# TensorE's order in the second half of an RWKV-7 recurrence written out by the kernel, with its inverse built from blocks of 16

## The chip, the cores and the metric

One core of a Trainium2 chip. The metric is the device time of one execution in microseconds (us). A core has TensorE (PE; its weight loads are shown as PEld), VectorE (DVE), ScalarE (ACT), GpSimd (POOL) and SyncE (SP), which issues the DMAs. Each engine runs its own list of instructions in order and waits for others by semaphores.

## The reference

One step of a two-layer streaming encoder over 1024 frames of a new stream and 64 frames of a running one, width 1024, 16 heads of 64. Layer 0 mixes by a recurrence and has a SwiGLU FFN (width 2816); layer 1 has sliding-window attention and an FFN. The recurrence:

```python
def step(s, inp):
    r_t, w_t, k_t, v_t, a_t, b_t = inp
    sa = jnp.einsum('bhvk,bhk->bhv', s, a_t)
    s = s * w_t[:, :, None, :] + sa[..., None] * b_t[:, :, None, :] + v_t[..., None] * k_t[:, :, None, :]
    return s, jnp.einsum('bhvk,bhk->bhv', s, r_t)
...
s_fin, y = lax.scan(step, s0.astype(f32), seq_in)
```

Its result y is normalised per head, gated, and goes through `rw_w_o` into the residual, then the FFN: `(silu(gu[..., :D_FF]) * gu[..., D_FF:]) @ w_out`.

## The kernel before, in words

The kernel is written on a framework whose planner orders the instructions: each carries a priority (`tc.cur_priority`, smaller is sooner), and a simulated timeline decides at compile time which ready instruction each engine takes next. What comes out is a fixed list for each engine.

The frames are cut into half A (chunks 0 to 7 of 64 frames) and half B (chunks 8 to 15 and, as chunk 16, the running stream). Dense products split each f32 operand into a high and a low part and take three PE instructions, lines 433 to 435 (`Dense.mm`): high x high, high x low, low x high. Weights come in pieces of 128 x 512 (`Dense.piece`: DMA on SP, cast on ACT at line 393, difference at line 394 on DVE or, every third time, POOL), three raw buffers and six split ones. Results go to three PSUM banks (`dp`).

The recurrence is `Rwkv`. Within a chunk of 64 frames it is a set of small products in f32 (line 73 for products, line 77 for transposes; PE takes each f32 product as two instructions, a transpose as one), and only the 64 x 64 state of each head goes from chunk to chunk. Its functions:

- `prep`: loads s, k, a, r of the chunk, norms of k (16 instructions of PE, tile `p_rp<-c_bd,r_rt`), decayed copies AR and BK on DVE, ACT and POOL, the 16 matrices X = BK AR (32 PE instructions, tile G) with a mask, and the bonus.
- `prep2`: `inverse`, which turns X's strictly triangular part of each head into W, and the transposes BT of BK. The inverse lays 32 x 32 blocks of all heads side by side on the partitions (ACT copies at line 190, a transpose on DVE), runs 15 steps of back substitution two columns at a time on DVE (products at line 215, reductions at 219, mostly in two parts each), and then joins the blocks of 32 to 64 by two groups of PE products with a copy between them.
- `chain`: the path from state to state. U0 from X and the state, U = W U0, then Sp from BT and U, and the new state M = (Sp + M) PC; beside it Y, the read-out (`seen`: 8 products of the old state for even heads, 8 for odd ones, with a memset on POOL, line 281, set between them; then 16 of U).
- `post`: the norm of Y per head on DVE, ACT and POOL, four transposes on PE, the gate, and the store of z to DRAM.

`recur` runs these over a list of chunks with two priorities, one for PE and one for the rest. The first half, chunks 0 to 7 (priority 1, its `prep` and `post` at 2.5), stands beside the r, k and v projections of half B (priority 2). The second half, chunks 8 to 16 (chain at 3, inverse at 3.1, `prep` and `post` of the other engines at 4.5), stands beside the dense work of half A at priority 4: `mixed_in("A")` loads z, `mix_out("A")` multiplies it by `rw_w_o` (8 groups of products, evacuation at line 898), `normed` makes the norm (squares at line 522, a sum over partitions at 532, its spread at 549, the scaled rows at 918), and `Ffn("A", 0).main` runs 22 times `up` (two halves of 8 products, evacuation at 941 to 945) and after every second one the `down` of an earlier pair (8 groups, evacuation into hx at 962). Which PE instruction comes next, one of the recurrence or a dense one, is the planner's choice alone. After that come `F.rest`, `mixed_in("B")` and the rest of the model, which need z of half B.

Buffers that the change touches: `rt` (three, for kkr, its square and P of `prep`), `yc` (one), `f4` (two of 4 KB a partition for the inverse), the PSUM banks `rp` (two), `rc` (two) and `ry` (one).

Of the kernel before, what the change touches and what calls it, by code (L numbers as in the profile page):

```python
# [46 lines left out]


class Rwkv:

# [31 lines left out]
    def start(self):  # L82

        nc = self.nc
        self.W = self.sb.tile([128, 8, 64], F32, name="W", tag="W", bufs=1)
        nc.gpsimd.memset(self.W, 0.0)

    def prep(self, ch):

# [12 lines left out]
        S.activation(sq, kkr, AF.Square)  # L102

        pn = self.pp()[0:64, 0:16].rearrange("p (par j) -> p par j", par=2)
        for j in range(8):
            self.mm(pn[:, :, j], lhsT=sq[:, j, :], rhs=c["bd"][:, 0:128:64], start=True, stop=True)
        n4 = self.t([128, 32], "n4")
        for q in range(4):
            d = 32 * (q % 2)
            V.tensor_scalar(out=n4[32 * q:32 * q + 32].rearrange("p (g j) -> p g j", g=4),  # L110
                            in0=mid(pn[d:d + 32, q // 2, :], 4), scalar1=1e-24, scalar2=None, op0=ALU.max)
        V.reciprocal(out=n4, in_=n4)
        nl = self.t([128, 32], "nl", 3)
        V.transpose(out=nl, in_=n4)


# [23 lines left out]
        G.tensor_tensor(out=kp, in0=kp, in1=bc(c["r_k"], 64), op=ALU.mult)  # L140


        X = self.t([128, 16, 128], "G", 2)
        flat2 = lambda x: x.rearrange("p a b -> p (a b)")
        for g in range(2):
            ps = [self.pp().rearrange("p (a b) -> p a b", a=4) for _ in range(2)]
            for i in range(4):
                for par in range(2):
                    h = slice(64 * par, 64 * par + 64)
                    self.mm(ps[par][:, i, :], lhsT=flat2(BK[h, 4 * g + i]), rhs=flat2(AR[h, 4 * g + i]), start=True, stop=True)  # L150
            for par in range(2):
                V.tensor_tensor(out=X[:, 8 * par + 4 * g:8 * par + 4 * g + 4, :], in0=ps[par], in1=mid(c["mask"], 4), op=ALU.mult)

        vf = self.t([128, 8, 64], "vf", 3)
# [3 lines left out]
        V.tensor_tensor(out=flat(vf), in0=pb, in1=flat(vf), op=ALU.mult)  # L158
        return dict(AR=AR, BK=BK, X=X, PC=PC, vf=vf, nl=nl)

    def prep2(self, d):
        nc = self.nc
        V, S = nc.vector, nc.scalar
        AR, X = d["AR"], d["X"]
        d["W"] = self.inverse(X, d["nl"])

        Xh = X.rearrange("p (par j) t -> p j par t", par=2)
        V.tensor_copy(Xh[0:64, :, 0, 0:64], AR[0:64, :, 0, :])
        S.copy(Xh[0:64, :, 1, 0:64], AR[64:128, :, 0, :])
        flat2 = lambda x: x.rearrange("p a b -> p (a b)")  # L170

        BT = d["BT"] = self.t([128, 16, 64], "BT")
        for g in range(2):
            ps = self.pp()
            for i in range(4):
                self.tr(ps[:, 128 * i:128 * i + 128], flat2(d["BK"][:, 4 * g + i]), self.c["id"])
            S.copy(flat2(BT[:, 8 * g:8 * g + 8, :]), ps)

    def inverse(self, X, nl):


        nc, c = self.nc, self.c
        V, S, G = nc.vector, nc.scalar, nc.gpsimd
        W = self.W
        Xh = X.rearrange("p (par j) t -> p j par t", par=2)
        st = self.t([128, 1024], "f4", 2)
        for q in range(4):
            d = 32 * (q % 2)
            src = Xh[d:d + 32, :, q // 2, d:d + 32].rearrange("p j t -> p t j").unsqueeze(2).broadcast_to([32, 32, 4, 8])
            S.copy(st[32 * q:32 * q + 32].rearrange("p (t g j) -> p t g j", g=4, j=8), src)  # L190
        N12 = self.t([128, 8, 32], "in12")
        S.copy(N12[0:32], Xh[0:32, :, 0, 32:64])
# [16 lines left out]
        for j in range(30, 0, -2):  # L209
# [3 lines left out]
            for h, r0 in part:  # L213
                n = 4 - r0
# [39 lines left out]
        V.tensor_copy(W[64:96, :, 32:64], ps[64:96])  # L254
        return W

    def chain(self, ch, d, M):
# [9 lines left out]
        E = lambda x: x.rearrange("p (a b) -> p a b", a=8)  # L267
        Y, U0p = E(self.p([128, 512], "ry", 1)), E(self.pc())
        X, BT, W = d["X"], d["BT"], d["W"]
        heads = [(i, i // 2, slice(64 * (i % 2), 64 * (i % 2) + 64)) for i in range(16)]  # L270
        for i, j, h in heads:
            self.mm(U0p[h, j, :], lhsT=X[:, 8 * (i % 2) + j, 0:64], rhs=sv[:, i, :], start=True, stop=True)


        out = lambda j, par: Y[64 * (j % 2):64 * (j % 2) + 64, j // 2 * 2 + par, :]

# [4 lines left out]
        by = G.memset(self.t([1, 1], "by", 2), 0.0)  # L281
        U0 = self.t([128, 8, 64], "yc")
        S.copy(U0, U0p)
        Up = E(self.pc())
        for i, j, h in heads:
            self.mm(Up[h, j, :], lhsT=W[h, j, :], rhs=U0[h, j, :], start=True, stop=True)
        V.tensor_copy(svh[0:64, :, 0, :], Up[0:64])
        S.copy(svh[0:64, :, 1, :], Up[64:128])
        Sp = E(self.pc())
        for i, j, h in heads:  # L290
            self.mm(Sp[h, j, :], lhsT=BT[:, i, :], rhs=sv[:, i, :], start=True, stop=True)

# [7 lines left out]
        Mn = self.t([128, 8, 64], "M", 2)  # L300
        V.tensor_tensor(out=Mn, in0=Sp, in1=M, op=ALU.add)
        V.tensor_tensor(out=Mn, in0=Mn, in1=bc(d["PC"], 64), op=ALU.mult)
        return Mn, Y

    def post(self, ch, d, Y):
        nc, c = self.nc, self.c
        V, S, G = nc.vector, nc.scalar, nc.gpsimd
# [14 lines left out]
        G.tensor_tensor(out=sm[:, 3, :], in0=sm[:, 2, :], in1=c["power"], op=ALU.pow)  # L322
        G.tensor_tensor(out=yc, in0=yc, in1=bc(sm[:, 3, :], 64), op=ALU.mult)

        for q in range(0, 8, 2):
# [25 lines left out]
class Dense:  # L351


    def __init__(self, tc, sb, ps, c):
        self.tc, self.nc, self.sb, self.ps, self.c = tc, tc.nc, sb, ps, c
        self.n = self.turn = 0
        self.more = self.esb = None
        self.mixed = []
        self.spare, self.early = deque("x" * RING), deque()
# [69 lines left out]
    def mm(self, ps, parts):  # L429

        last = len(parts) - 1
        for i, (wh, wl, xh, xl) in enumerate(parts):
            self.nc.tensor.matmul(ps, lhsT=wh, rhs=xh, start=i == 0, stop=False)  # L433
            self.nc.tensor.matmul(ps, lhsT=wh, rhs=xl, start=False, stop=False)  # L434
            self.nc.tensor.matmul(ps, lhsT=wl, rhs=xh, start=False, stop=i == last)  # L435

    def full(self, src, xs, groups, evac):
# [135 lines left out]
def tile_stream_step(ctx: ExitStack, tc: tile.TileContext, I, O):  # L573
# [278 lines left out]
    def all(gen):  # L852
        for _ in gen:
            pass
# [138 lines left out]
    def prio(p):  # L993
        tc.cur_priority = int(p * 1000000)
# [36 lines left out]

    def recur(chunks, M, base, low):

        rw.two.at(base, base)
        d = rw.prep(chunks[0])
        rw.prep2(d)
        for i, ch in enumerate(chunks):
            nd, late = None, 0.001 * i
            if i + 1 < len(chunks):
                rw.two.at(base + 0.301 + late, low + 0.301 + late)  # L1040
                nd = rw.prep(chunks[i + 1])
            rw.two.at(base + late, base + late)
            M, Y = rw.chain(ch, d, M)
            rw.two.at(base + late, low + late)
            rw.post(ch, d, Y)
            if nd:
                rw.two.at(base + 0.1 + late, base + 0.1 + late)
                rw.prep2(nd)
            d = nd
        return M  # L1050

    M = recur(range(8), M, 1, LOW[0])
    prio(2)
# [6 lines left out]
    all(rkv("B", "k", xs["Bk"]))  # L1060
    prio(3)
    M = recur(range(8, 16), M, 3, LOW[1])
    nc.sync.dma_start(O["wkv_p"], M.rearrange("p a b -> p (a b)"))
    M = rw.t([128, 8, 64], "M", 2)
    nc.sync.dma_start(M.rearrange("p a b -> p (a b)"), I["s0"])
    M = recur([16], M, 3.5, LOW[1] + 0.4)
    nc.sync.dma_start(O["wkv_s"], M.rearrange("p a b -> p (a b)"))
    prio(4)
# [5 lines left out]
    F = Ffn("A", 0, xA, x0)  # L1074
    all(F.main())
    rctx.close()
# [351 lines left out]
```

## Time and profile before

| | |
|---|---|
| median of 3 runs | 3046.8 us (3043.08 to 3048.04) |
| profiled execution | 3042.33 us, span 3040.6 us |
| mean granted clock of PE | 0.961 |
| PE busy | 2854.4 us (94%) |
| DVE busy | 1885.7 us (62%) |
| ACT, POOL busy | 1371.7 us (45%), 920.5 us (30%) |
| line 190 (ACT copies of the inverse) | 135.8 us, 68 times |
| lines 215 and 219 (DVE steps of the inverse) | 119.4 and 98.7 us, 476 times each |

How to read it: the span is the time from the first to the last instruction of one profiled execution, the execution's own time is a little longer. Busy times of engines overlap. Ends of PE instructions are modelled, so that consecutive products overlap in the list and start-to-start distances say more than durations. A row of a group gives line, engine, operation, tiles (out <- in), count, busy time and mean, and then how long the engine stood idle before and what ended that. The granted clock is the share of full speed at which PE was allowed to run.

### The profile page before, as it was taken

The numbers are of one execution on the slowest core, as the hardware profiler recorded it, in microseconds if no ns is written. First come the engines' busy times: TensorE is split into PE (matmuls) and PEld (weight loads), VectorE is DVE, ScalarE is ACT, GpSimd is POOL, SyncE is SP. The second block draws the span as 40 slices with busy tenths as digits, with TensorE's granted clock in tenths as the row PEclk, the third lists the DMA queues.
The fourth block names the chain that finished last, engine by engine and source line by source line (L and its number), as shares of the span: only waits on it lengthen the run. The fifth ranks groups of instructions, "written<-read, shape, count | busy, mean of one in ns | idle before, by whom it ended". The sixth has DMA issues, their size and how long they took to land. (4 is left out here: it accounts for less than half of the span.)

```text
span 3040.6 us, 51529 instructions
## 1 busy us (share of the span) xinstructions
PE 2854.4 (94%) x19650; PEld 2463.5 (81%) x19650; DVE 1885.7 (62%) x3964; ACT 1371.7 (45%) x2491; POOL 920.5 (30%) x785
## 2 busy tenths in 40 slices
PE   6998888988899999999999999999999999999998
PEld 5677777876677777887789999888777888999998
DVE  8887788968998994357554333565554335533334
ACT  6866665545545542244653222344554233322222
POOL 6555124333333332224211222243111222322221
PEclk9999778988899999999999999999999999999999
DMA  4645353344232225332212222222222332322222
GB/s 145 169 124 148 112 144 93 108 118 133 78 95 88 89 69 137 100 114 80 70 49 63 84 84 84 77 85 79 65 67 74 94 94 80 105 84 84 84 84 70
DMA packets 262048, 289.10 MB, mean 95 GB/s; under 512 B 125029, under 2 KB 143973, under 8 KB 261801
## 3 DMA queue, kind: packets, MB, share of 16 engines
q1 hardware_dynamic: 261800, 285.81, 31.7%
q8 instruction: 154, 2.52, 0.4%
q14 instruction: 94, 0.76, 0.1%
HBM read 243.18 MB, written 41.16 MB: 94 GB/s over the span
## 5 line engine op out<-in xcount | busy, mean ns | idle before, releaser
L433 PE MATMUL dp<-xh,wh 128*128 128x288 f32 (+2 forms) x3480 | 1180.3, 340 | 29.2 <-DVE hx L962 11.4
L434 PE MATMUL dp<-xl,wh 128*128 128x288 f32 (+2 forms) x3480 | 1172.0, 337 | 9.7 <-POOL xl L426 6.5
L435 PE MATMUL dp<-xh,wl 128*128 128x288 f32 (+2 forms) x3480 | 1167.9, 336 | 0.0
L393 ACT CAST wh<-wr 128x512 fp32r<-128x512 f32 x730 | 446.0, 619 | 820.4 <-PE dp L434 613.5
L433 PEld LDWEIGHTS dp<-xh,wh 128*128 128x128 f32 x3480 | 665.6, 192 | 109.9 <-DVE hx L962 16.0
L434 PEld LDWEIGHTS dp<-xl,wh 128*128 128x128 f32 x3480 | 666.0, 191 | 74.6 <-issue 8.6
L435 PEld LDWEIGHTS dp<-xh,wl 128*128 128x128 f32 x3480 | 666.2, 191 | 60.3 <-issue 4.9
L394 POOL TENSOR_TENSOR wl<-wr,wh 128x512 fp32r<-128x512 f32 x243 | 340.2, 1400 | 1063.2 <-ACT wh L393 948.7
L394 DVE TENSOR_TENSOR wl<-wr,wh 128x512 fp32r<-128x512 f32 x487 | 374.6, 772 | 421.1 <-ACT wh L393 417.0
L433 PE MATMUL dp<-mh,wh 128*128 128x288 f32 (+1 forms) x808 | 254.5, 315 | 0.2 <-DVE hx L962 0.2
L435 PE MATMUL dp<-mh,wl 128*128 128x288 f32 (+1 forms) x808 | 254.0, 314 | 0.0
L434 PE MATMUL dp<-ml,wh 128*128 128x288 f32 (+1 forms) x808 | 253.8, 314 | 0.0
L962 DVE TENSOR_TENSOR a_xB<-dp,a_xB 128x288 f32<-128x288 f32 x352 | 157.7, 455 | 83.5 <-PE dp L435 82.8
L943 DVE TENSOR_TENSOR st<-st,dp 128x288 f32<-128x288 f32 (+1 forms) x132 | 70.0, 530 | 222.0 <-PE dp L435 221.6
L945 POOL TENSOR_TENSOR xl<-st,xh 128x288 fp32r<-128x288 f32 (+1 forms) x102 | 102.2, 1002 | 327.6 <-ACT xh L944 318.8
L433 PEld LDWEIGHTS dp<-mh,wh 128*128 128x128 f32 x808 | 152.5, 189 | 10.7 <-issue 3.0
L435 PEld LDWEIGHTS dp<-mh,wl 128*128 128x128 f32 x808 | 152.6, 189 | 8.5 <-issue 2.4
L434 PEld LDWEIGHTS dp<-ml,wh 128*128 128x128 f32 x808 | 152.6, 189 | 6.8 <-issue 1.1
L190 ACT COPY r_f<-r_G 32x1024 f32<-32x1024 f32 x68 | 135.8, 1997 | 37.4 <-DVE r_f L226 25.4
L962 DVE TENSOR_TENSOR hx<-dp,hx 128x512 f32<-128x512 f32 x176 | 119.7, 685 | 47.9 <-PE dp L435 47.3
L215 DVE TENSOR_TENSOR r_f<-r_f,r_f 128x60 f32<-128x60 f32 (+5 forms) x476 | 119.4, 282 | 0.5
L944 ACT CAST xh<-st 128x288 fp32r<-128x288 f32 (+1 forms) x102 | 50.2, 492 | 137.3 <-DVE st L943 136.3
(343 smaller groups left out, 3850.3 us busy)
## 6 DMA issues: line engine op xcount, KB each, us to landing
wr<-in_ffn_in SPq DMA_DIRECT2D x352, 256.0 KB
wr<-in_ffn_out SPq DMA_DIRECT2D x176, 256.0 KB
wr<-in_rkv SPq DMA_DIRECT2D x90, 256.0 KB
wr<-in_rwo SPq DMA_DIRECT2D x32, 256.0 KB
wr<-in_wq SPq DMA_DIRECT2D x32, 256.0 KB
wr<-in_wo SPq DMA_DIRECT2D x32, 256.0 KB
r_r_s<-s_s SPq DMA_DIRECT2D x17, 256.0 KB
r_sv<-s_vt SPq DMA_DIRECT2D x17, 256.0 KB
```

The source lines that it names most:

```text
L190: S.copy(st[32 * q:32 * q + 32].rearrange("p (t g j) -> p t g j", g=4, j=8), src)
L215: V.tensor_tensor(out=Z[:, h, 1:3, r0:4, 0:j], in0=Z[:, h, a, r0:4, j:j + 2].rearrange("p r c -> p c r").unsqueeze(3).broadcast_to([128, 2 ...
L393: nc.scalar.copy(h, x)
L394: (nc.gpsimd if self.turn % 3 == 0 else nc.vector).tensor_tensor(out=l, in0=x, in1=h, op=ALU.subtract)
L433: self.nc.tensor.matmul(ps, lhsT=wh, rhs=xh, start=i == 0, stop=False)
L434: self.nc.tensor.matmul(ps, lhsT=wh, rhs=xl, start=False, stop=False)
L435: self.nc.tensor.matmul(ps, lhsT=wl, rhs=xh, start=False, stop=i == last)
L943: V.tensor_tensor(out=t[o], in0=t[o], in1=p, op=ALU.mult)
L944: S.copy(a.hi[:, q], t[o])
L945: G.tensor_tensor(out=a.lo[:, q], in0=t[o], in1=a.hi[:, q], op=ALU.subtract)
L962: V.tensor_tensor(out=self.x[m][:, q], in0=p, in1=self.x[m][:, q], op=ALU.add)
```

## The change

The two halves get functions of their own. `recur_free` is the old `recur` for chunks 0 to 7. For chunks 8 to 16 a new `recur` is a generator that issues one group of the recurrence, yields the time of dense work that is to pass, and goes on. The new class `Pump` holds it: from `pump.start` on, PE's order is that in which the kernel issues the instructions (`manual_schedule` for PE alone; the other engines stay with the planner), and `Dense.mm` tells it after every three products how much dense time has gone by. Products that don't go through `Dense.mm`, those of the norms, do not tick.

```diff
+class Pump:
+    def start(self, gen, priority):
...
+            self.region = self.tc.manual_schedule(engines={mybir.EngineType.PE})
+            self.region.__enter__()
+        self.tick(0)
...
+    def tick(self, n):
+        if self.gen is None:
+            return
+        self.need -= 0.44 * n + 6
+        while self.gen is not None and self.need <= 0:
+            self.step()
...
             self.nc.tensor.matmul(ps, lhsT=wl, rhs=xh, start=False, stop=i == last)
+            if self.pump:
+                self.pump.tick(3 * ps.shape[1])
...
-LOW = (2.5, 4.5)
+LOW = 2.5
+FREE = (1.5, 5.0)
...
+    def recur(chunks, M, base, low, scale, free, ends):
...
+        us = 1000.0
+        inv, fill = low + 0.05, low + 0.2
...
+        def turns(g, v, p):
+            for gap in (1.2, 1.4, 1.2, 1.4):
+                for x in (g, v):
+                    if x and next(x, x) is not x:
+                        yield gap * scale * us
+        load(0, base)
+        yield 16 * us
+        step(gs[0], base)
+        yield 4 * us
+        rw.two.at(inv, inv)
+        yield from turns(gs[0], None, base)
+        inverse(0, base)
+        keys(0, base)
+        load(1, inv)
+        yield 12 * us
+        step(gs[1], inv)
+        yield 4 * us
+        rw.two.at(inv, inv)
+        yield from turns(gs[1], vs[0], inv)
+        inverse(1, inv)
+        old = None
+        for i, ch in enumerate(chunks):
+            g, v = None, vs.get(i + 1)
+            k = rw.chain(ch, ds[i], M)
+            step(k, base)
+            yield 1.8 * scale * us
+            step(k, base)
+            if old:
+                step(old, fill)
+            yield 1.8 * scale * us
+            step(k, base)
+            M = ds[i]["M"]
+            if i + 1 < len(chunks):
+                yield scale * us
+                keys(i + 1, inv)
+            if i + 2 < len(chunks):
+                load(i + 2, inv)
+                g = gs[i + 2]
+            yield 2 * scale * us
+            step(k, base)
+            yield 1.6 * scale * us
+            step(k, base)
...
+            old = rw.post(ch, ds[i])
+            step(old, fill)
+            yield 2 * scale * us
+            if g:
+                step(g, inv)
+                yield 2 * scale * us
+            rw.two.at(inv, inv)
+            yield from turns(g, v, inv)
+            if i + 2 < len(chunks):
+                inverse(i + 2, inv)
+            yield free * us
+        step(old, fill)
...
-    M = recur(range(8), M, 1, LOW[0])
+    M = recur_free(range(8), M, 1, LOW)
...
+    pump.start(recur(range(8, 17), M, 3, 4, *FREE, {
+        15: saved, 16: lambda M: nc.sync.dma_start(O["wkv_s"], M.rearrange("p a b -> p (a b)"))}), 3)
```

`prep`, `chain` and `post` become generators that stop between their groups of PE instructions. In `prep` the products for the norms of k come after the rest of the DVE work; in `chain`, for both halves, the new state is issued before the read-out, and U0 takes a buffer of `rt` instead of `yc`. `turned` is the part of `prep2` that makes BT (`keys` calls it).

The second half takes a new `inverse16` in the place of `inverse` (which stays, as `inverse32`, for the first). It lays blocks of 16 on the partitions, two masks of which are made once at the start (`self.e`, `self.xl`), needs 7 steps of one product and one reduction each, and joins 16 to 32 by two groups of 32 products on PE, and 32 to 64 as before:

```diff
+        for j in range(14, 0, -2):
+            a, b = (0, 3) if j % 4 else (3, 0)
+            r0, n = j // 2, 8 - j // 2
+            V.tensor_tensor(out=Z[:, 1:3, r0:8, 0:j],
...
+            V.tensor_reduce(out=Z[:, b, r0:8, 0:j], ...
...
+        for j in range(8):
+            for q in range(4):
+                o = slice(32 * q, 32 * q + 32)
+                self.mm(ps[o, j, :], lhsT=T(q, j, slice(o.start % 64, o.start % 64 + 32)), rhs=XD[o, j, 0:16], start=True, stop=True)
+        S.copy(Q1[:, :, 0:16], ps)
+        yield
...
+                self.mm(ps[o, j, :], lhsT=Q1[o, j, :], rhs=WD[o, j, 16:32], start=True, stop=True)
+        V.tensor_tensor(out=WD[:, :, 16:32], in0=ps, in1=WD[:, :, 16:32], op=ALU.add)
+        turn()
```

More of the change, by code (lines that the diff above doesn't have):

```diff
@@ L84, in start, with prep @@
         nc = self.nc
-        self.W = self.sb.tile([128, 8, 64], F32, name="W", tag="W", bufs=1)
-        nc.gpsimd.memset(self.W, 0.0)
-    def prep(self, ch):
+        V, G = nc.vector, nc.gpsimd
+        one = lambda shape, n: self.sb.tile(shape, F32, name=n, tag=n, bufs=1)
+        self.W = one([128, 8, 64], "W")
+        G.memset(self.W, 0.0)
+        self.e = one([128, 8], "lanes")
+        for i, w in ((0, 16), (2, 32), (4, 8)):
+            for h in range(2):
+                V.tensor_reduce(out=self.e[:, i + h:i + h + 1], in_=self.c["id"].rearrange("p (a h w) -> p a h w", h=2, w=w)[:, :, h, :],
+                                axis=AX.XY, op=ALU.add)
+        self.xl = one([128, 8, 16], "xl")
+        G.memset(self.xl, 0.0)
+        for g in range(2):
+            V.tensor_copy(self.xl.rearrange("p a b -> p (a b)")[:, g:128:18], self.e[:, 4 + g:5 + g].broadcast_to([128, 8]))
+    def prep(self, ch, d, wide=False):
         nc, c = self.nc, self.c
@@ L102, in prep @@
         S.activation(sq, kkr, AF.Square)
[L104 to L114, printed above, removed]
         IP, P = s, self.tmp(65)
@@ L158, in prep, with turned @@
         V.tensor_tensor(out=flat(vf), in0=pb, in1=flat(vf), op=ALU.mult)
[L159 to L170, printed above, removed]
+        d["vf"] = vf
+        yield
+    def turned(self, d):
         BT = d["BT"] = self.t([128, 16, 64], "BT")
@@ L281, in chain @@
         by = G.memset(self.t([1, 1], "by", 2), 0.0)
[L282 to L291, printed above, removed]
+        yield
         odd = seen(1)
@@ L299, in chain, with post @@
                 self.mm(out(j, par), lhsT=X[:, 8 * par + j, 64:128], rhs=sv[:, 2 * j + par, :], start=False, stop=q == 6 and par == 1)
[L300 to L306, printed above, removed]
+        d["Y"] = Y
+        yield
+    def post(self, ch, d):
+        nc, c, Y = self.nc, self.c, d["Y"]
         V, S, G = nc.vector, nc.scalar, nc.gpsimd
@@ L1030, in tile_stream_step, with recur_free, prep, prep2 @@
     G.memset(M, 0.0)
-    def recur(chunks, M, base, low):
+    def recur_free(chunks, M, base, low):
+        def prep(i):
+            all(rw.prep(chunks[i], ds[i], wide=True))
+        def prep2(i):
+            rw.inverse32(ds[i])
+            rw.turned(ds[i])
+        ds = [{} for _ in chunks]
         rw.two.at(base, base)
-        d = rw.prep(chunks[0])
-        rw.prep2(d)
+        prep(0)
+        prep2(0)
         for i, ch in enumerate(chunks):
-            nd, late = None, 0.001 * i
+            late = 0.001 * i
@@ L1039, in recur @@
             if i + 1 < len(chunks):
                 rw.two.at(base + 0.301 + late, low + 0.301 + late)
-                nd = rw.prep(chunks[i + 1])
+                prep(i + 1)
             rw.two.at(base + late, base + late)
-            M, Y = rw.chain(ch, d, M)
+            all(rw.chain(ch, ds[i], M))
+            M = ds[i]["M"]
             rw.two.at(base + late, low + late)
-            rw.post(ch, d, Y)
-            if nd:
+            all(rw.post(ch, ds[i]))
+            if i + 1 < len(chunks):
@@ L1047, in recur, with step, load, inverse @@
                 rw.two.at(base + 0.1 + late, base + 0.1 + late)
-                rw.prep2(nd)
-            d = nd
-        return M
-    M = recur(range(8), M, 1, LOW[0])
+                prep2(i + 1)
+        return M
+    def recur(chunks, M, base, low, scale, free, ends):
+        def step(g, p):
+            rw.two.at(p, p)
+            next(g)
+        us = 1000.0
+        inv, fill = low + 0.05, low + 0.2
+        chunks, ds, gs, vs = list(chunks), [{} for _ in chunks], {}, {}
+        def load(i, p):
+            gs[i] = rw.prep(chunks[i], ds[i])
+            step(gs[i], p)
+        def inverse(i, p):
+            vs[i] = rw.inverse16(ds[i])
+            step(vs[i], p)
+        def keys(i, p):
+            rw.two.at(p, p)
+            rw.turned(ds[i])
+        def turns(g, v, p):
[29 more added lines that the diff above has]
+            step(k, base)
+            M = ds[i]["M"]
+            if i + 1 < len(chunks):
+                yield scale * us
[7 more added lines that the diff above has]
+            step(k, base)
+            if ch in ends:
+                M = ends[ch](M)
+            old = rw.post(ch, ds[i])
+            step(old, fill)
+            yield 2 * scale * us
+            if g:
+                step(g, inv)
[6 more added lines that the diff above has]
+        step(old, fill)
@@ L1060, in tile_stream_step, with saved @@
     all(rkv("B", "k", xs["Bk"]))
[L1061 to L1067, printed above, removed]
+    pump = dn.pump = Pump(tc)
+    def saved(M):
+        nc.sync.dma_start(O["wkv_p"], M.rearrange("p a b -> p (a b)"))
+        M = rw.t([128, 8, 64], "M", 2)
+        nc.sync.dma_start(M.rearrange("p a b -> p (a b)"), I["s0"])
+        return M
+    pump.start(recur(range(8, 17), M, 3, 4, *FREE, {
+        15: saved, 16: lambda M: nc.sync.dma_start(O["wkv_s"], M.rearrange("p a b -> p (a b)"))}), 3)
     prio(4)
@@ L1074, in tile_stream_step @@
     F = Ffn("A", 0, xA, x0)
-    all(F.main())
+    for _ in F.main():
+        if pump.region and not pump.gen:
+            pump.end()
     rctx.close()
```

159 lines of the change are left out of this document (148 added, 11 removed).

## The prediction

> **What bounds it.** I read the page's busy lines and its slices, then busy time by stage, then the timeline at the ends of the stages. On the page:
>
> ```profile
> PE 2854.4 (94%) x19650; PEld 2463.5 (81%) x19650; DVE 1885.7 (62%) x3964; ACT 1371.7 (45%) x2491; POOL 920.5 (30%) x785
> DVE  8887788968998994357554333565554335533334
> PEclk9999778988899999999999999999999999999999
> ```
>
> TensorE (PE) is the busiest engine, but in slices 4 to 15 of 76 us each VectorE (DVE) stands mostly at 8 or 9 tenths and PE's granted clock below full. These hold the two halves of the recurrence. The stage of the second half begins and ends here:
>
> ```profile
> 685.54 1.12 PE L73 MATMUL p_ry<-r_M,r_AR 64*64 64x64 f32 x16
> 686.14 0.62 ACT L425 CAST xh<-hx 128x512 fp32r<-128x512 f32 x1 [8.52 <-DMA hx<-s_z]
> 686.81 1.22 PE L433 MATMUL dp<-xh,wh 128*128 128x512 f32 x2
> 1308.96 0.69 DVE L943 TENSOR_TENSOR st<-st,dp 128x512 f32<-128x512 f32 x1 [1.72 <-PE dp L435]
> ```
>
> At 686.8 us the first dense product of `mix_out("A")` starts, held until then by the load of z; at 1309.5 the last `up` of the first FFN is read out. Chunks 8 to 16 run between. Busy time by stage (us, then PE, PEld, DVE, ACT, POOL, clock, DMA):
>
> ```profile
> 660.00:686.80 26.80, 15.36 (x152) 13.21 (x150) 16.07 (x31) 6.46 (x12) 9.84 (x10) 0.61 0.49 132
> 686.80:771.00 84.20, 69.78 (x408) 52.75 (x410) 70.81 (x165) 43.53 (x59) 27.52 (x19) 0.84 0.44 121
> 771.00:1190.00 419.00, 386.11 (x3318) 301.55 (x3316) 365.92 (x926) 202.87 (x282) 150.57 (x119) 0.94 0.28 86
> 1190.00:1309.50 119.50, 119.50 (x518) 96.93 (x517) 44.33 (x67) 34.72 (x57) 26.53 (x22) 1.00 0.44 124
> 686.80:1309.50 622.70, 575.39 (x4236) 451.23 (x4237) 481.07 (x1157) 281.12 (x397) 204.62 (x160) 0.94 0.34 98
> 290.00:663.00 373.00, 330.07 (x3412) 290.93 (x3410) 309.32 (x873) 224.47 (x358) 118.31 (x97) 0.87 0.40 113
> ```
>
> From 1190 on there is dense work alone: 119.50 us over 518 products is 0.2307 us each, PE without a gap. The code has 64 groups of three products in `mix_out`, 352 in `up` and 160 in `down`, 576 in all: 1728 x 0.2307 = 398.6 us. The same view for single lines (columns PE, PEld): three rows for line 73 and two for line 77, the recurrence's own products, and one for line 433, the first of each group of three:
>
> ```profile
> 660.00:686.80 26.80, 13.60 (x144) 12.12 (x144) 0.61 0.49 132
> 771.00:1190.00 419.00, 111.56 (x2202) 92.79 (x2199) 0.94 0.28 86
> 686.80:1309.50 622.70, 124.05 (x2386) 102.36 (x2386) 0.94 0.34 98
> 771.00:1190.00 419.00, 13.91 (x92) 10.39 (x92) 0.94 0.28 86
> 686.80:1309.50 622.70, 16.82 (x108) 12.68 (x108) 0.94 0.34 98
> 771.00:1190.00 419.00, 147.80 (x342) 68.20 (x342) 0.94 0.28 86
> ```
>
> In the whole stretch the recurrence takes 124.1 + 16.8 = 140.9 us. What is left of 622.7 is 83 us in which PE waits or runs at half clock; the clock row alone accounts for (1 - 0.94) x 622.7 = 37 us of it. Of the 83, 57 fall between 771 and 1190 (419.0 less 342 x 3 x 0.2307 = 237 of dense work and 111.6 + 13.9 = 125 of recurrence), and the other 26 before 771. So PE's own work is already 540 of 623 us, and the change can win only out of the 83.
>
> **The change, part by part.** *Inverse by blocks of 16.* On DVE and ACT (17 chunks; for lines 215, 219 and 190 the busy sums):
>
> ```profile
> L190 ACT COPY r_f<-r_G 32x1024 f32<-32x1024 f32 x68 | 135.8, 1997 | 37.4 <-DVE r_f L226 25.4
> L215 DVE TENSOR_TENSOR r_f<-r_f,r_f 128x60 f32<-128x60 f32 (+5 forms) x476 | 119.4, 282 | 0.5
> L219 DVE TENSOR_REDUCE r_f<-r_f 128x30 f32<-128x90 f32 (+5 forms) x476 | 98.7, 237 | 0.5
> ```
>
> These are 8.0 us of ACT and 7.0 + 5.8 us of DVE a chunk. The new loop has 7 steps of one product and one reduction, 14 instructions instead of 56: at 0.28 and 0.24 us that is 3.6 us instead of 12.8. The four copies, the transpose and the scalings work on half the elements: about 4 us of ACT and 3 of DVE less; the lane masks, the second turn and the sum from PSUM put some 1.5 us of DVE back. Estimate: 11 us of DVE a chunk less, 100 us over nine chunks, so DVE goes from 481 of 623 us to about 380. By itself this moves no end: PE is the longer engine. What it buys is that evacuations and the recurrence's steps are less late.
>
> On PE the inverse gets dearer. Before it is two groups of 16 products (32 instructions); now there are two of 32 and two of 16. Price and changeover:
>
> ```profile
> 847.06 0.40 PE L433 MATMUL dp<-xh,wh 128*128 128x512 f32 x1
> 847.29 0.40 PE L434 MATMUL dp<-xl,wh 128*128 128x512 f32 x1
> 847.62 0.69 PE L73 MATMUL p_rc<-r_ixd,r_in 32*32 32x32 f32 x32
> 848.25 0.50 PE L435 MATMUL dp<-xh,wl 128*128 128x512 f32 x1
> 1032.46 0.50 PE L433 MATMUL dp<-xh,wh 128*128 128x512 f32 x1
> 1032.80 0.39 PE L434 MATMUL dp<-xl,wh 128*128 128x512 f32 x1
> ```
>
> A group of 32 instructions lasts 848.25 - 847.62 = 0.63 us, of which 0.11 is the way out (below), so a group of 64 lasts 1.15. Per chunk 2 x 1.15 more and nothing taken away: +2.3, times 9 = +20 us. Products of this form on four tiles have no row; the bounds are half of that and the same; I take the same, since a product's two passes follow each other on one tile. [...] No row here shows four tiles at once. [...]
>
> *Order fixed, wide room.* Going into a group costs 0.33 - 0.23 = 0.10 us, coming out 0.34 - 0.23 = 0.11. The kernel now issues about 14 separate groups a chunk, 126 in all; before, the planner let several run back to back. If a third were merged, 42 more changes x 0.21 = 9 us. Chunk 8's preparation and read-outs ran in the hole before 686.8 (13.6 us busy at clock 0.61, 8.3 at full clock, a little of it chunk 7's) and now stand in the fixed order: +7 us. The gaps themselves cost nothing: they are the dense products, which must run anyway, at 0.23 us. The sum of the yields is 55 us at the start, 36.8 for each of seven chunks, 28 and 19 for the last two, about 360 of some 393 us in the kernel's own tally of dense time, so the recurrence ends before `F.main` does, and z is there for `mixed_in("B")`. A chunk's four loads on SP and its preparation now rank behind the dense weights (4.05 against 4.0):
>
> ```profile
> L101 POOL TENSOR_TENSOR r_rt<-r_r_k,vecs 128x512 f32<-128x512 f32 x17 | 21.8, 1281 | 36.8 <-DMA r_r_k<-s_k 36.7
> ```
>
> POOL waits about 2 us a chunk for the first of them. They may start when their buffers are free, most of a period (37 us of dense work and a chunk's own groups) ahead of the product that needs them, so I cost them at nothing; without that lead PE would wait those 2 us a chunk, 18 in all.
>
> The fixed order also takes something away. When a group is late, everything behind it on PE is late: dense products, hence evacuations, hence PSUM banks and the weights' buffers. And where the dense side waits, no recurrence can be put in. That place is the norm between `mix_out` and the FFN:
>
> ```profile
> 756.02 0.40 PE L435 MATMUL dp<-xh,wl 128*128 128x512 f32 x1
> 762.65 0.63 ACT L522 ACTIVATE st<-hx 128x512 f32<-128x512 f32 x1 [1.57 <-DVE hx L898]
> 764.80 1.86 PE L532 MATMUL dp<-ones,lo 128*128 128x1 f32 x8
> 768.48 2.07 PE L549 MATMUL dp<-lo,ones 128*128 128x512 f32 x2
> 772.93 0.96 PE L433 MATMUL dp<-xh,wh 128*128 128x512 f32 x3
> ```
>
> From the square at 762.65 to the first FFN product is 10.3 us, and before it comes one evacuation of 0.7; the planner put chunk 8's chain into it. Fixed, PE idles about 11 us there, and some 4 more while the eight normed rows arrive and the clock recovers: 15 us. The start, where the eight rows of z come one by one, costs about 8. Together 23 against the 26 lost before 771 now: no gain there.
>
> So the gain is in the 57 us. The longest named waits of PE between 771 and 1190 are
>
> ```profile
> PE dp L433 <- DVE hx L962: 5.7, 4, 2.8
> PE p_ry L73 <- POOL r_by L281: 4.6, 4, 2.0
> ```
>
> (total, times, longest). What stands in front of them on their engines:
>
> ```profile
> L283 ACT COPY r_yc<-p_rc x8: 571/586/591, 825.3 to 1161.2; 128x512 f32<-128x512 f32 x8
> L962 DVE TENSOR_TENSOR hx<-dp,hx 128x512 f32<-128x512 f32 x176 | 119.7, 685 | 47.9 <-PE dp L435 47.3
> L945 POOL TENSOR_TENSOR xl<-st,xh 128x288 fp32r<-128x288 f32 (+1 forms) x102 | 102.2, 1002 | 327.6 <-ACT xh L944 318.8
> ```
>  Gaps of 1.8 to 3 us between a group and the one that needs its result cover a copy of 0.6 us behind one or two others, so most waits go, and the half clock that follows them. Bounds: 5 us are left (one late evacuation or memset for every two chunks) or all 57 stay. I take 14, near the low end, since the waits that remain in a fixed order are of the kind of these two rows and DVE is less full. On the clock: it stood at 0.94 although no named wait was over 2.8 us. [...]
>
> *First half.* `recur_free` keeps its arithmetic. The next state is issued ahead of the read-out (16 instructions less on the chain; 1.12 us at half clock at 685.54, so 0.6), the sums for the norms come later, and U0 moves from a buffer it shared with `post` to the three buffers of `prep`. Set-up adds eight small DVE instructions, 2 us once at line 219's 0.24. In 290 to 663 DVE is busy 309 of 373 us, so order moves little; bounds -5 (the shorter chain, eight times) and +15 (U0 waits 2 us a chunk for a buffer); I take 0. Without the preparation of chunk 9 and the inverse of chunk 8 on DVE and ACT, the dense start comes about 2 us sooner: -2.
>
> *Sum.* 398.6 + 140.9 + 20 + 9 + 7 + 23 + 14 = 612.5 against 622.7: -10, with the start -12. The profiled execution took 3042.3 us (span 3040.6); the median of the runs is 3046.8, 4.5 above. So 3030 for a profiled execution, 3035 for the median.
>
> **The rivals.** (1) *The waits vanish almost wholly*, and the groups of 64 last as long as those of 32 (0.63 us): 9 + 9 us less, and the first half's shorter chain up to 5: about 3015. For it: the pure dense stage shows that PE in program order loses nothing. Against: the POOL memset between the two read-outs stays, and POOL's operations are over 1 us long. (2) *Nothing changes*: waits go, but the extra products, changes and the norm gap eat them (36 us of added PE work against some 31 to 43 saved). That needs 26 us of waits left; 3047. (3) *Slower: a fixed order exposes each late group.* Place: the 126 changes between 771 and the end. Price: if groups are late by 0.25 us on average, 32 us are left and the change is slower; at the full 57 it is +31, 3078. For it: the DVE share in `down` is high, as each evacuation takes 0.69 us for six products of 0.23, and the planner's order on DVE and ACT is still made on its own times. [...] Against: DVE sheds 100 us. Middle of this case: 3064.
>
> **How the numbers follow.** My sum: 34%. Rival 1: 18%. Rival 2: 20%. Rival 3: 28%. Below 0.2% (6 us) this kernel can't be told from no change. Faster: 34 + 18 = 52%; same 20%; slower 28%. The range runs from rival 1 less the first half's bound (3008) to most of rival 3 (3073); within the faster cases alone it is 3008 to 3041.
>
> **What would show it.** Right: PE clock 1.00 between the norm and the end of `F.main`; DVE near 60% there; recurrence groups of lines 73 and 77 spread evenly to about 40 us before the last `up`; an idle stretch of 11 us on PE around the norm's two products; the 64-instruction groups at 1.1 us; first start to last `up` in about 612 us. Wrong: PE waits named by a copy on ACT or DVE at many groups, a clock below 0.94 in that stretch, or a first half whose last z is stored more than 5 us away from where it is now.

## The result, and the profile after

| | before | after |
|---|---|---|
| median of the runs, same chip (20 runs each) | 3044.1 us | 3052.3 us |
| ratio, 95% interval | | 1.0025, 1.0017 to 1.0032 |
| profiled execution (span) | 3042.3 (3040.6) us | 3049.6 (3047.8) us |
| first dense product of the stage to the read-out of its last `up` | 686.8 to 1309.0: 622.2 us | 683.7 to 1305.9: 622.2 us |
| from there to the end of the span (below: the rest) | 1731.6 us | 1741.9 us |

The changed kernel is 8 us slower; 12 us less were forecast. (The experiments ran on several chips; a ratio is always against the kernel before on the same chip.) The changed stage did not get shorter by a microsecond, and 10 us more were spent behind it, in code that the change does not touch. In what follows line 604 to 606 of the kernel after are the three dense products (433 to 435 before), and 109 and 113 the recurrence's products (73 and 77 before).

Busy time of the engines and the slices of DVE and the clock, from the page of the kernel after:

```profile
PE 2849.6 (93%) x20802; PEld 2455.3 (81%) x20802; DVE 1828.2 (60%) x3630; ACT 1342.9 (44%) x2485; POOL 911.8 (30%) x795
DVE  8887789967777676457654333565554345533334
PEclk9999878988999999999999999999999999999999
```

In the changed stage (slices 10 to 17) DVE has come down where it stood at 9 tenths, as the change means it to. Busy time by stage, kernel after (columns as in the forecast: us, then PE, PEld, DVE, ACT, POOL, clock, DMA), and the same stretch for line 109 and for line 113 alone:

```profile
683.60:770.00 86.40, 75.45 (x468) 55.23 (x469) 62.41 (x110) 37.14 (x58) 26.50 (x18) 0.87 0.41 119
770.00:1190.00 420.00, 387.25 (x4008) 300.17 (x4007) 292.38 (x603) 181.62 (x277) 136.55 (x122) 0.95 0.29 89
1190.00:1306.20 116.20, 113.94 (x995) 90.43 (x994) 60.99 (x113) 33.69 (x59) 32.79 (x29) 0.99 0.42 115
683.60:1306.20 622.60, 576.64 (x5467) 445.82 (x5468) 415.79 (x825) 252.46 (x392) 195.84 (x169) 0.95 0.33 98
290.00:663.00 373.00, 323.86 (x3371) 287.00 (x3369) 319.39 (x872) 221.70 (x353) 122.70 (x98) 0.86 0.40 112
683.60:1306.20 622.60, 124.59 (x3618) 102.44 (x3618) 0.95 0.33 98
683.60:1306.20 622.60, 15.39 (x108) 12.23 (x108) 0.95 0.33 98
```

The sum of the forecast can be made again: 622.6 us are 398.6 of dense products, 124.6 + 15.4 = 140.0 of recurrence, and 84.0 of waiting, half clock and the few products of the norm. The last is what it was before (83). DVE shed 65 us in the stage (481.1 to 415.8), and the stage is no shorter. PE's waits in that stretch (total, times, longest) name the reason:

```profile
PE p_rc L109 <- DVE r_ixd L404: 23.9, 8, 4.2
PE dp L604 <- ACT xh L596: 13.0, 2, 10.9
PE p_ry L109 <- POOL r_by L459: 8.1, 5, 2.3
PE p_rp L109 <- DVE r_n L187: 3.2, 1, 3.2
```

The second row is the norm's gap. The first is new in its size: line 404 is `V.tensor_copy(QT[96:128], ps[96:128])`, the copy between the third and the fourth group of the inverse. The kernel before has the same copy, line 247, and waited for it 2.7 us between 771 and 1190 (the row stands further down). One of the eight places in the timeline, PE first, then ACT, then DVE:

```profile
888.38 0.19 PE L109 MATMUL p_rc<-r_ixd,r_in 32*32 32x32 f32 x1
888.50 0.50 PE L604 MATMUL dp<-xh,wh 128*128 128x512 f32 x1
890.77 0.24 PE L109 MATMUL p_rc<-r_ixd 32*32 32x32 f32 x2
895.22 1.05 PE L109 MATMUL p_rc<-r_ixd 32*32 32x32 f32 x30 [4.21 <-DVE r_ixd L404]
896.21 0.80 PE L604 MATMUL dp<-xh,wh 128*128 128x512 f32 x1
889.28 0.36 ACT L403 COPY r_ixd<-p_rc 32x256 f32<-32x256 f32 x1
888.64 0.68 DVE L1135 TENSOR_TENSOR hx<-dp,hx 128x512 f32<-128x512 f32 x1
...
894.43 0.28 DVE L343 TENSOR_TENSOR r_f<-xl,r_nl 128x128 f32<-128x128 f32 x1
894.74 0.43 DVE L404 COPY r_ixd<-p_rc 32x256 f32<-32x256 f32 x1
```

The third group ends at 888.6. Its first half is copied on ACT at once (889.28). Its second half stands on DVE behind eleven other instructions (read-outs of `down`, weight differences, the preparation and the inverse of later chunks) and is copied at 894.74. The fixed order leaves nine dense products, 2.1 us, between the groups; after them PE stands 4.21 us, and the next dense product takes 0.80 us, at half clock, instead of 0.40.

### The profile page after: what moved, and what is told of

Its sections match the earlier page's. It is cut to its first block, busy times and chain, and to the rows that moved or that the text cites. A ratio compares the mean times of both kernels' runs of the same rounds, so it can differ in the third digit from the quotient of the medians.

```text
span 3047.8 us, 53525 instructions
## 1 busy us (share of the span) xinstructions
PE 2849.6 (93%) x20802; PEld 2455.3 (81%) x20802; DVE 1828.2 (60%) x3630; ACT 1342.9 (44%) x2485; POOL 911.8 (30%) x795
## 5 line engine op out<-in xcount | busy, mean ns | idle before, releaser
L604 PE MATMUL dp<-xh,wh 128*128 128x288 f32 (+2 forms) x3480 | 1194.8, 344 | 34.6 <-ACT xh L596 15.1
L565 POOL TENSOR_TENSOR wl<-wr,wh 128x512 fp32r<-128x512 f32 x243 | 333.5, 1372 | 1055.1 <-ACT wh L564 965.0
L1114 ACT ACTIVATE st<-dp 128x288 f32<-128x288 f32 (+1 forms) x132 | 62.1, 470 | 92.5 <-PE dp L606 92.1
L597 POOL TENSOR_TENSOR xl<-st,xh 128x512 fp32r<-128x512 f32 (+2 forms) x37 | 64.7, 1759 | 70.2 <-ACT xh L596 66.2
```

Of the source, the lines that this page charges most:

```text
L565: (nc.gpsimd if self.turn % 3 == 0 else nc.vector).tensor_tensor(out=l, in0=x, in1=h, op=ALU.subtract)
L597: (eng or self.nc.vector).tensor_tensor(out=lo, in0=x, in1=hi, op=ALU.subtract)
L1114: S.activation(t[o], p, AF.Silu)
```

## The experiments

**Two ways to take the late copy away.** First the copy on the other engine:

```diff
-        V.tensor_copy(QT[96:128], ps[96:128])
+        S.copy(QT[96:128], ps[96:128])
```

> The copy of the third group's second half (QT[96:128]) goes to ScalarE instead of VectorE; nothing else. Theory A (one late copy): the 23.9 us that TensorE waited for that copy, eight times some 3 us, come back, and with them the half-clock windows that followed each; the stage of 622 us falls to 580 to 600 us and the whole kernel to about 3010 to 3030 us. Rival B (the time is VectorE's): VectorE's queue is what is late, so the next result of VectorE that TensorE needs is waited for instead; stage 612 to 622 us, kernel 3042 to 3052 us.

Measured: 3014.2 us, ratio to before 0.9903 (0.9886 to 0.9920); stage 592.4 us (686.5 to 1278.9). Then the copy left on DVE, with room in front of the last group instead:

```diff
-            for gap in (1.2, 1.4, 1.2, 1.4):
+            for n, gap in enumerate((1.2, 1.4, 1.2, 1.4)):
...
-                        yield gap * scale * us
+                        yield gap * scale * us + (5 * us if x is v and n == 2 else 0)
...
-FREE = (1.5, 5.0)
+FREE = (1.5, 0.0)
```

> The copy stays on VectorE, but 5 us more of dense products stand between the third and the fourth group of the inverse, taken from the 5 us of room that end each chunk's turn. Theory A (one late copy, too little room): the wait for it falls from 23.9 us to under 6, stage 585 to 605 us, kernel 3015 to 3035 us. Rival B (the time is VectorE's): the wait moves to another VectorE result of the inverse or of the chain, stage 612 to 625 us, kernel 3042 to 3055 us.

Measured: 3018.8 us, ratio 0.9913 (0.9898 to 0.9928); stage 593.7 us. The longest waits that are left with the copy on ScalarE, and its stage as a whole, then the stage with more room:

```profile
PE dp L604 <- ACT xh L596: 13.1, 2, 11.0
PE p_ry L109 <- POOL r_by L459: 7.9, 5, 2.0
PE p_rp L109 <- DVE r_n L187: 3.2, 1, 3.2
686.50:1278.90 592.40, 563.77 (x5466) 435.47 (x5467) 409.89 (x816) 255.45 (x400) 198.67 (x169) 0.97 0.34 103
688.70:1282.40 593.70, 562.45 (x5466) 434.18 (x5467) 420.77 (x824) 252.06 (x391) 200.06 (x169) 0.98 0.34 103
```

The row of the copy is gone, and none of its size took its place: the largest that are new are 3.1 us (three waits for line 441 on ACT) with the copy on ScalarE and 4.3 us (three waits for line 1116 on DVE) with more room. The stage falls by 29.8 us: 23.9 of named wait, and the clock, whose row goes from 0.95 of 622.6 (31 us below full) to 0.97 of 592.4 (18 us); the two overlap. Two edits that share nothing but the lateness of one copy give the same stage within 1.3 us. Theory A is shown, B fell.

**Each part of the change alone.** The inverse by 16 with the planner's order (the second part runs through `recur_free` with its priorities of before, and `inverse16` in place of `inverse32`):

> The inverse by blocks of 16 stays, but the order on TensorE is the planner's again, as in the kernel before. Theory A (the fixed order brings the stalls on the late copy, the inverse by 16 only relieves VectorE): stage 600 to 615 us, kernel 3022 to 3037 us. Rival C (the inverse by 16 brings what the fixed order saves): stage 625 to 640 us, kernel 3048 to 3065 us. If the stage stays at 622 us, neither part moves it by itself and the limit is in what both leave alone.

Measured: 3024.6 us, ratio 0.9936 (0.9920 to 0.9952); stage 599.3 us, what theory A gave and a little better. Then the fixed order with the inverse by 32, cut into steps at the places where `inverse16` is cut. A first version of it wrote the diagonal blocks of W a chunk too early, so that its W was another one:

> TensorE's order stays fixed by the kernel, with the same room, but the inverse of the second part is the one by blocks of 32 again (VectorE some 65 us more in this stage, two TensorE groups of 64 fewer for each chunk). Theory A: the copy is as late or later, since VectorE is busier; its wait is 24 to 45 us, stage 622 to 645 us, kernel 3050 to 3075 us. Rival C (the inverse by 16 is what costs): two groups and their changeovers fewer, stage 605 to 618 us, kernel 3035 to 3045 us.

Measured: 3141.1 us, ratio 1.0316 (1.0299 to 1.0333); stage 714.9 us, outside both ranges (622 to 645 and 605 to 618). PE's longest wait there:

```profile
PE p_rc L109 <- ACT W L293: 57.7, 8, 9.4
```

This is the misplaced write. The version without it:

```diff
-        for q in range(4):
-            f = (q % 2) * 32
-            e = V.tensor_copy if q % 2 else S.copy
-            e(W[32 * q:32 * q + 32, :, f:f + 32], WD[32 * q:32 * q + 32])
         yield
         yield
+        for q in range(4):
+            f = (q % 2) * 32
+            e = V.tensor_copy if q % 2 else S.copy
+            e(W[32 * q:32 * q + 32, :, f:f + 32], WD[32 * q:32 * q + 32])
         yield
```

> As the third kernel (fixed order, inverse by blocks of 32), but the diagonal blocks of W are written with the step in which the inverse by 16 writes them. In the third kernel they were written a chunk too early (so its W was another one) and TensorE waited 57.7 us for them. Theory A (late VectorE work in a fixed order; inverse by 32 has more of it): the waits for the two copies of the third group (28.7 and 19.3 us there) stay, the 57.7 us go; stage 640 to 665 us against 622 us, kernel 3065 to 3090 us. Rival C (the inverse by 16 is what costs): stage 605 to 618 us, kernel 3030 to 3045 us.

Measured: 3075.4 us, ratio 1.0101 (1.0088 to 1.0114); stage 651.2 us, inside what theory A gave. Both copies of the third group are waited for here, the one on ACT too, 48 us in all as in the first version:

```profile
PE p_rc L109 <- DVE r_ixd L303: 28.7, 8, 5.1
PE p_rc L109 <- ACT r_ixd L302: 19.4, 8, 5.5
686.00:1337.20 651.20, 572.08 (x4314) 443.26 (x4315) 487.93 (x1167) 287.09 (x400) 195.46 (x161) 0.92 0.31 93
686.00:1337.20 651.20, 115.64 (x2466) 95.03 (x2466) 0.92 0.31 93
```

(the last row is line 109). The stage in the four combinations:

| | inverse by 32 | inverse by 16 |
|---|---|---|
| planner's order | 622.2 us | 599.3 us |
| fixed order | 651.2 us | 622.2 us |

The inverse by 16 saves 23 us in one order and 29 in the other; the fixed order with this room costs 29 us with one inverse and 23 with the other. Two of the four differences are of one part alone: 23 us for the order (with the inverse by 16) and 29 us for the inverse (with the fixed order). The first cell is the kernel before, which also lacks what the other three share: the new state issued ahead of the read-out, the sums for the norms of k later, and U0 in another buffer. No run has these edits alone, so their share in the other two differences is not shown. The changed kernel is in the main the sum of a gain and a loss of the same size.

**What is left in the stage.** The recurrence let into the norm's gap (the copy on ScalarE in all that follows here):

```diff
             xs.append(dn.split(x, eng=G if j % 2 else V))
+            if dn.pump:
+                dn.pump.tick(3200)
             yield
```

> The copy on ScalarE, and while the norm ahead of the feed-forward part scales its eight tiles, the recurrence's groups are let in as if 1.4 us of dense products had gone by for each tile. Theory: the 11 us in which TensorE waits for the first split tile and the half clock behind it are filled with recurrence; stage 576 to 586 us against 592 us, kernel 2996 to 3008 us. Rival (the groups' own inputs are late there, since VectorE is busy with the norm): the wait only changes its name, stage 588 to 595 us, kernel 3010 to 3020 us.

Measured: 3018.0 us, ratio 0.9920 (0.9905 to 0.9936); stage 596.8 us. A miss: the groups got in, PE waits for them instead, and the stage is 4.4 us longer than without (592.4).

```profile
760.39 2.04 PE L109 MATMUL p_rp<-r_rkr,c_bd 128*128 128x512 f32 x2 [1.75 <-DVE r_G L210]
769.77 0.26 PE L109 MATMUL p_rc<-r_ixd,r_G 32*32 32x32 f32 x1 [7.33 <-DVE r_ixd L369]
771.96 1.44 PE L109 MATMUL p_rc<-r_ixd 32*32 32x32 f32 x32 [1.13 <-ACT r_ixd L403]
```

The third group needs the turn of line 369 from DVE, and that stood behind the norm's own work (the scalings of line 1091 and the splits of line 597): the rival had the mechanism, though the stage lies 1.8 us above its range. On top of that, more room ahead of the odd heads' products:

```diff
-            yield 1.6 * scale * us
+            yield 2.6 * scale * us
```

> As the kernel with the norm's gap filled, and 1.5 us more of dense products between the even and the odd heads' share of the output, so that the small GpSimd memset between them is no longer waited for (7.9 us in five waits). If those waits and the half clock behind them cost what they look like: stage 4 to 10 us below the kernel with the gap filled alone. If longer recurrence cycles bring nothing, because the time is set elsewhere: within 3 us of it.

Measured: 3013.8 us, ratio 0.9900 (0.9886 to 0.9914); stage 591.1 us, 5.7 below, as expected; the row of line 459 is gone. So the same without the norm's part:

> The copy on ScalarE, and 1.5 us more room ahead of the odd heads' products, the norm's gap left alone. The recurrence's waits for the small memset (7.9 us) go, with the half clock behind them: stage 584 to 589 us against 592 us, kernel 3004 to 3012 us with a rest of 1731 to 1736 us, up to 3018 us with one of 1742 us.

Measured: 3010.4 us, ratio to before 0.9876 (0.9862 to 0.9889); stage 586.0 us, as expected, and the fastest version that was run. Between the norm and the last chunk it looks as the forecast had hoped for the change itself:

```profile
770.00:1190.00 420.00, 407.06 (x4263) 314.38 (x4263) 314.50 (x647) 195.99 (x304) 147.42 (x129) 0.99 0.31 95
1190.00:1270.30 80.30, 80.30 (x745) 63.95 (x742) 37.42 (x58) 23.43 (x41) 26.23 (x23) 1.00 0.49 133
```

**The 10 us behind the stage.** There PE's instructions are the same in the same order. Two stretches of 40 us hold nearly all of the loss (5.1 and some 5 us, by the starts of PE's instructions): right behind the stage, and 1255 to 1295 us after its end. Rows of before, after, then the two kernels with the late copy cured by ScalarE and by room (first stretch, second stretch):

```profile
1309.00:1349.00 40.00, 36.47 (x229) 32.34 (x228) 28.87 (x45) 19.82 (x33) 7.83 (x6) 1.00 0.42 131
2564.00:2604.00 40.00, 34.85 (x173) 27.21 (x172) 33.45 (x46) 19.26 (x33) 17.01 (x10) 1.00 0.22 70
1305.90:1345.90 40.00, 34.49 (x190) 30.36 (x189) 27.04 (x41) 17.74 (x30) 6.57 (x5) 0.91 0.48 153
2560.90:2600.90 40.00, 35.44 (x160) 28.19 (x160) 29.52 (x40) 15.83 (x28) 11.40 (x7) 0.87 0.17 53
1278.90:1318.90 40.00, 35.85 (x213) 31.30 (x212) 28.69 (x44) 19.76 (x34) 8.32 (x6) 0.96 0.46 152
2533.90:2573.90 40.00, 34.85 (x173) 27.25 (x172) 33.44 (x46) 19.04 (x33) 16.78 (x10) 1.00 0.20 66
1282.40:1322.40 40.00, 34.51 (x202) 30.40 (x201) 27.29 (x41) 18.45 (x31) 7.31 (x6) 0.96 0.47 152
2537.40:2577.40 40.00, 35.85 (x170) 28.36 (x169) 28.99 (x42) 16.25 (x28) 12.80 (x8) 0.91 0.17 55
```

It is mostly the clock: 1.00 in both before, 0.91 and 0.87 after. Up to 1720 us after the end of the stage the records show 20 us of half clock before and 37 after, which is 8.5 of the 10 us. At the head of the second stretch PE waits as long in both kernels for the norm of one tile, and falls to half clock in one of them (before, then after; the ten products take 1.26 and 1.73 us):

```profile
2570.41 1.26 PE L532 MATMUL dp<-ones,lo 128*128 128x1 f32 x10 [1.45 <-DVE lo L524]
2572.11 1.73 PE L705 MATMUL dp<-ones,lo 128*128 128x1 f32 x10 [1.45 <-DVE lo L697]
```

The last two kernels of the table say the same: behind the stage the order on PE, DVE, ACT and POOL is the same in both, yet their rests take 1732.6 and 1739.7 us. In the clock records of the kernel before and of the changed kernel every change lies within 0.005 us of a grid of 3.41 us; so, does the half clock depend on where that grid falls? The changed kernel once more:

> The changed kernel once more, for a second profile of the same program. Theory P (in which of the clock's windows of 3.41 us a gap falls is chance): the 1741.9 us that its unchanged rest took in the first profile, 10 us more than in the kernel before, come out otherwise here, 1732 to 1739 us, with fewer half-clock windows than the 38 us there. Theory S (the rest is slower by its order on the engines): 1740 to 1744 us again. The stage 618 to 626 us by either.

Measured: 3053.1 us, ratio 1.0022 (1.0012 to 1.0031); rest 1741.6 us, with the granted clock in the two stretches at 0.91 and 0.87 again. That is against theory P, but two profiles don't rule chance out: the ten executions of this run took 3042.2 to 3054.7 us, a spread larger than the loss. Then the code was moved against the grid by products without effect, ahead of the stage's last tile:

```diff
+                    if self.first and f == NF - 1 and half and o == self.groups[-1][0]:
+                        for _ in range(7):
+                            nc.tensor.matmul(p, lhsT=dn.part(w, 0, 128)[0], rhs=xs[0].hi[:, q], start=True, stop=True)
                     dn.mm(p, [(*dn.part(w, k * 128, 128), x.hi[:, q], x.lo[:, q]) for k, x in enumerate(xs)])
```

> The changed kernel with seven more products of 512 columns, which do nothing, ahead of the last `up` tile of the changed stage: 7 x 0.231 = 1.6 us more work, about half of a clock window of 3.41 us. Theory W (the place of the clock's windows against the code, 3.0 us into a window at the end of the stage in both profiles of the changed kernel, makes its rest slow): the rest falls from 1741.7 us to 1732 to 1736 us, and the kernel comes out 4 to 8 us faster than the changed kernel, in spite of the added work. Theory S (order on the engines alone): rest 1740 to 1744 us, kernel 1 to 2 us slower.

Measured: 3051.4 us, ratio 1.0011 (1.0000 to 1.0022), 3 to 4 us under the changed kernel's 1.0022 and 1.0025, where theory W had 4 to 8; rest 1734.1 us in the profile, in the changed kernel's own order on the other engines but for two instructions in the first 17 us. The stretches:

```profile
1309.00:1349.00 40.00, 35.80 (x213) 31.30 (x213) 27.60 (x43) 19.37 (x33) 8.34 (x6) 0.96 0.44 136
2564.00:2604.00 40.00, 34.64 (x168) 27.80 (x166) 32.95 (x46) 17.94 (x31) 17.06 (x10) 0.96 0.21 61
```

> The same with fifteen products, 3.46 us, about one whole window: the code stands against the windows as without them. Theory W: rest 1740 to 1743 us again, kernel 3 to 4 us slower than the changed kernel. If the delay as such or the changed plan did the good (or harm), the rest would be as with seven.

Measured: 3050.7 us, ratio 1.0011 (1.0002 to 1.0020); rest 1734.2 us, where theory W had 1740 to 1743. But the longer kernel also got another plan: some twenty instructions of DVE, ACT and POOL in the second stretch stand as in the kernel before again, so the run changed two things.

> The kernel before with six such products (1.38 us) at the same place: by the place of its windows (1.6 us into one at the end of the stage) this brings it to 3.0 us, where the changed kernel stands. Theory W: its rest, 1731.6 us, becomes 1735 to 1742 us, the kernel 5 to 11 us slower than before. Theory S: rest 1731 to 1733 us, kernel 1 to 2 us slower.

Measured: 3048.2 us, ratio 1.0000 (0.9989 to 1.0010); rest 1731.7 us; theory W had 1735 to 1742. The stage itself came out 0.8 us shorter, its end stood 1.3 us into a window and not 3.0, so the condition was not met.

What follows: the 10 us are mostly half clock, and one order of instructions can take 7 to 8 us more or less in single profiles (the two cured kernels; nearly one order with seven products). That the place on the grid decides it is not shown. The profile with seven products is the fastest of its twelve executions (3044.9 us, median 3051.4), the one with fifteen the fastest of eleven (3046.9, median 3050.7), and the cured kernel with more room was profiled in the slowest of five (3023.9, median 3018.8). In the medians the ratio falls only from 1.0025 to 1.0011, and the intervals touch. The place alone does not sort the rests either: the end of the stage stands 2.1 us into a window in the cured kernel with more room, with a rest of 1739.7 us, and 2.2 us in the one with the planner's order, with 1730.9 us. The latter has the order of the kernel before behind the stage, and so has the kernel before with six products (1731.7 us); the fastest version has the order of the two cured ones, and its rest is 1735.6 us. How much of the 8 us is the grid, how much the other order of some twenty instructions 1270 us later, and how much chance, stays open.

## Why the prediction was wrong, by its own steps

The sum had two large errors that nearly cancelled, and a third place that it did not look at. That its 612.5 us lie within 10 us of the measured 622.2 is luck.

- *DVE.* About 380 were forecast, 415.8 came. In the stage the busy times of lines 215 and 219 add up to 117.6 us, as the forecast counted them, but their instructions overlap in the trace: together the two lines were busy for 104.2 us, and the new loop for 34.3. That is 7.8 us a chunk, not 9.2. The lane masks, the second turn and the sum from PSUM were put at 1.5 us a chunk; these three rows alone (kernel after, nine chunks) are 2.7, where the one turn before took 0.4:

```profile
L363 DVE TENSOR_SCALAR r_f<-r_f,lanes 128x128 f32<-128x128 f32 x18 | 8.7, 524 | 0.2
L369 DVE STREAM_TRANSPOSE r_ixd<-r_ixd 128x256 f32<-128x256 f32 x18 | 7.9, 436 | 0.3
L334 DVE SCALAR_TENSOR_TENSOR r_f<-r_f,lanes 128x256 f32<-128x256 f32 x9 | 7.3, 813 | 0.0
```

- *PE's added work, 20 + 9 + 7 = 36 us.* The recurrence's own busy time does not show it: 140.9 became 140.0. With the order fixed in both, inverse by 32 against by 16, line 109 goes from 115.64 to 124.59: 9 us for 18 groups of 64, not 20. One of them in full, 0.65 us from its start to that of the next product, where a group of 32 took 0.63 before and 1.15 were taken:

```profile
882.70 0.73 PE L109 MATMUL p_rc<-r_ixd 32*32 32x16 f32 x64
883.35 0.50 PE L604 MATMUL dp<-xh,wh 128*128 128x512 f32 x1
```

  Of the two bounds beside this term the lower, half of it, was the better estimate: 10 us. The 9 us of changes between groups lie outside these rows and were not measured apart.
- *The waits that are left, 14 us: the step that failed.* Worked out for the kernel after as the forecast did it for the one before (74, 371 and 133 groups of dense products before 770, up to 1190 and behind), waiting and half clock are 22, 56 and 5 us. The first is the start and the gap of the norm, where 23 were taken (the norm's wait is 10.9 us where 11 was said). The second was 57 and should have fallen to 14: it did not fall. One copy made 23.9 us of it by name, and with its half clock 30. The forecast had the mechanism as its rival 3, with place and price (late groups in a fixed order, slower from 32 us on), and gave it 28%. It argued from gaps of 1.8 to 3 us that "cover a copy of 0.6 us behind one or two others". At the place shown the copy of line 404 stood behind eleven. The rows of before could have told. The forecast looked at the two longest waits between 771 and 1190, for an evacuation and a memset; below them stand the results of the inverse, and among them this very copy (line 247), with DVE busy 366 of 419 us:

```profile
PE p_rc L73 <- DVE r_ixd L236: 4.4, 3, 2.5
PE p_rc L73 <- ACT r_ixd L246: 3.0, 2, 2.2
PE p_rc L73 <- DVE r_ixd L247: 2.7, 2, 1.5
```

- *DVE relief moves no end by itself.* This does not stand: with the planner's order the inverse by 16, with the smaller edits that came with it, moved the stage by 23 us, and in the fixed order the inverse alone moved it by 29. That the lighter DVE is the reason is likely, since the waits named in the fixed order with the inverse by 32 are for copies, but a lighter DVE was not tried without the new inverse.
- *The start, -2, and the first half, 0.* Not decided: the stage starts 3.1 us sooner in one profile of the changed kernel and 1.8 us later in the other (683.7 and 688.6 against 686.8).
- *Behind the stage.* The forecast summed nothing there. This is where the net 8 us lie. Rival 2 ("nothing changes") describes the stage to the tenth of a microsecond, by coincidence of a gain and a loss, and still misses the kernel.
- *What would show it.* Clock 1.00 in the FFN part: 0.95. DVE near 60% there: 70% (292.4 of 420). About 612 us: 622. The recurrence 40 us ahead of the last `up`: its last z is stored at 1287.9, 18 us ahead. "PE waits named by a copy on ACT or DVE at many groups" was put down as the sign of error, and that is what came.

## What to carry to other kernels

When an engine's order is fixed by hand, list for each group which engine makes its input, and how many instructions stand ahead of it in that engine's queue; the room needed is that queue, not the one instruction. A result needed within 2 us may belong on an engine with a shorter queue; here ACT, busy 252 of 623 us, cured the wait. A low share is not enough by itself: with the inverse by 32 the half of the copy that stood on ACT was waited for too (19.4 us, eight times). A higher priority on DVE was not tried. And try the parts of a change one by one: here one was worth 23 to 29 us and the other cost as much, and one copy moved decided between them.

## What the runs showed of the hardware

Half clock followed grid steps in which PE stood idle for only part of the time. In the profiles of the kernel before and of the kernel after, the granted clock takes two values, 1.0 and 0.5. Cut both into the 3.41 us steps of their own clock records, and add up PE's idle time between its matmuls in each step (their ends are modelled). Of 1443 full-clock steps with under 0.25 us idle 2 were followed by half clock; of 76 with 0.25 to 1.0 us 3; of 47 with 1.0 to 1.5 us 11; of 20 with 1.5 to 2.0 us 12; of 40 with 2.0 us or more all 40. The gap of 1.45 us shown above is among these: before, 1.33 us of it fell into one step, and the clock stayed full; after, all of it did, and 6.8 us of half clock followed.

Whether that place is drawn anew each time was seen in two profiles only. Those of the changed kernel reach the stage 4.9 us apart (683.7 and 688.6), and from there agree within 0.3 us in the length of the stage (622.2 and 621.9) and of the rest (1741.9 and 1741.6), with the same granted clock in the two stretches above (0.91 and 0.87). Why they agree was not tested.
